# Feed-forward value chunks by seven block products instead of eight, in a fused two-model kernel on one core

## The chip, the core and the metric

One core of one Trainium2 chip runs the whole program: two small transformer blocks one after the other, batch 1, 512 tokens, model width 1024, all in float32. The metric is the device time of one execution in microseconds (us). The engines are TensorE (PE, matmuls; PEld is its weight load), VectorE (DVE), ScalarE (ACT), GpSimd (POOL) and SyncE (SP, here only a DMA queue). Each takes its own instructions in the order in which they were written.

## The reference, cut to what matters

The change lies in the feed-forward, which runs twice (layers 0 and 1 of the first block):

```python
def conv_ffn(x, w_up, conv_w, conv_b, w_down):      # x: 512 x 1024, w_up: 1024 x 5632, w_down: 2816 x 1024
    a, g = jnp.split(x @ w_up, 2, axis=-1)           # values a, gates g: 512 x 2816 each
    g = lax.conv_general_dilated(g, conv_w[:, None, :], (1,), ((2, 0),), ..., feature_group_count=D_FF) + conv_b
    return (jax.nn.gelu(g) * a) @ w_down
```

The result is added to alpha times x and goes through a layer norm. The order of the program is: even mixer, feed-forward 0, odd mixer, feed-forward 1, and then a gated linear recurrence and a retention layer.

## The kernel before, in words

Every product is made of three matmuls. A float32 operand is split into hi (a rounded copy, on ACT) and lo (the rest, a subtraction on DVE), and `mm3` (L273) adds hi times hi, hi times lo and lo times hi. X^T, the input with its 1024 features on partitions (8 k-tiles of 128) and its 512 tokens on columns, is kept as `xh` and `xl`.

**Weights.** `unit` lists a load of up to 1 MB into one of two raw buffers (`NRAW`), and `piece` one half of it (8 k-tiles x 128 columns, 1024 elements a partition) that is split into hi and lo. `pump` (L180) walks both lists as far as it can: a load is issued on SP as soon as the unit two places ahead of it has no piece left, and a piece is split (`split_piece`, L238 on ACT, L242 on DVE) while fewer than 5 split pieces are held. `get` (L254) gives up the pieces of the last chunk, pumps, and returns the next ones. As engines are in order, a split stands in ACT's and DVE's queues behind the work that was written before that `get`.

**Feed-forward** (`ffn`, L1127). The 22 chunks of 128 features are taken in pairs: two gate chunks, then the two value chunks of the same features. A chunk is 8 k-tiles x 3 matmuls of 512 columns into one of the 8 PSUM banks (`fm`, L281). `g_evac` (L1132) takes a gate chunk out of PSUM: ACT scales it (L1137), DVE adds the two shifted products of the convolution (L1138, L1139), ACT applies the gelu (L1140). `a_evac` (L1143) multiplies the value chunk by it on DVE (L1145) and splits the result into hi and lo (L371 ACT, L372 DVE). The first four chunks run in two halves of 256 tokens, as the transposed tokens of the layer norm before come in (`fms` with `split`, L291). After the first 12 chunks the down projection adds their part to the residual (`tm`, two halves of 512 columns); the last 10 go through `out_proj` (L1045), whose second half runs token tile by token tile (`tail=5`: 5 weight pieces of 2 chunks held), with the layer norm of each tile following on DVE, ACT and POOL (L403, L415 to L425, and for layer 1 also a root-mean-square norm, L443 to L451) and its transposes at `middle()` and after the last tile. After the first part the kernel also issues loads of the norm's parameters on ACT's queue (L430), in layer 1 the parameters of the recurrence (`lru_params`, L1787, a chain of small DVE operations with one exponential on ACT) and in layer 0 one table copy on POOL's queue (L531).

In the feed-forwards POOL has nothing to do except the layer norms at either end.

Of the kernel before, what the change touches and what calls it, by code (L numbers as in the profile page):

```python
# [28 lines left out]
SPL = 4  # L29
# [84 lines left out]
class Core:  # L114
# [4 lines left out]
    def __init__(self, ctx, tc, io):  # L119
# [16 lines left out]
        self.next_raw = self.next_piece = self.cur = 0  # L136
        self.live = deque()
        self.nm = 0
        self.pending = deque()
# [35 lines left out]

    def piece(self, u, view, a, b, direct=False):
        self.units[u]["left"] += 1
        self.plist.append((u, view, a, b, direct))

    def pump(self, split=True):  # L180
        while True:
# [13 lines left out]
            n = self.next_piece  # L195
            if split and n < len(self.plist) and self.room():
                u, view, a, b, direct = self.plist[n]
# [53 lines left out]
    tight = spare = extra = 0  # L251
    held = 0

    def get(self, n=1):  # L254

# [9 lines left out]
        self.held = n  # L265
        self.pump()
        assert len(self.live) >= n
# [4 lines left out]

    def mm3(self, out, lhs, rhs, start, stop):  # L273
        (lh, ll), (rh, rl) = lhs, rhs
        mm = self.T.matmul
        mm(out, lh, rh, start=start, stop=False)  # L276
        mm(out, lh, rl, start=False, stop=False)  # L277
        mm(out, ll, rh, start=False, stop=stop)  # L278

# [10 lines left out]

    def fms(self, evacs, split=0):  # L291


        n = 0
        if split:
            self.flush(1)
            self.extra, self.eager = 0, False
            ws = self.get(split)
            pss = [self.ps() for _ in ws]
            for t0 in (0, 256):  # L300
                for k, (w, p) in enumerate(zip(ws, pss)):
                    if t0 or k == split - 1:
                        self.flush(3 if t0 else 2)
                    yield from self.fm(p, w, t0=t0, t1=t0 + 256)
                    if t0:
                        evacs[k](p)
                        if k == EAGER:
                            self.eager = True
                            self.pump()
            n = split  # L310
        for f in evacs[n:]:
            w, = self.get()
            p = self.ps()
            yield from self.fm(p, w)
            f(p)

    def tm(self, lhs, kpers, n, done, tail=3, pack=False, kind="mm", before=None, extra=2, middle=None):
# [809 lines left out]
    def ffn(self, l, rms=False):  # L1127
        A, V, al, fr = self.A, self.V, self.al, self.fr
        self.pool_lo = False
# [4 lines left out]
        def g_evac(c, p):  # L1134
# [8 lines left out]
        def a_evac(c, p):  # L1143
            acc = H[c]
            V.tensor_tensor(acc, p, acc, op=MUL)  # L1145
            hi, lo = al(F32R), al(F32R)
            self.split(hi, lo, acc)
            fr(acc)
            H[c] = hi, lo

        for part in self.FF_PARTS:
            fs = []
            for j in range(c0, c0 + part, 2):
                fs += [lambda p, c=c: g_evac(c, p) for c in (j, j + 1)] + [lambda p, c=c: a_evac(c, p) for c in (j, j + 1)]
            run(self.fms(fs, split=SPL if c0 == 0 else 0))
            if c0 == 0:
                gb = self.norm_params(l, 1)
                if rms:
                    g = self.bcast(self.io["norm_pre_2"][0])
                    self.lru_params()  # L1160
                if l == 0 and self.pre_rms:
                    self.table(4)
            lhs = lambda k, i: [t[:, i * 128:i * 128 + 128] for t in H[c0 + k]]
            first = c0 == 0
            if first:
                for h in range(2):
                    run(self.tm(lhs, [2] * (part // 2), 512, lambda i, p, h=h: self.residual(i, h, p), tail=0))
# [968 lines left out]
```

## Time and profile before

| | |
|---|---|
| median of 3 runs | 2002.61 us (2000.42 to 2003.55) |
| the profiled execution, its own time | 1997.43 us |
| its span, first to last instruction | 1995.5 us |
| busy share: PE, DVE, ACT, POOL | 98%, 50%, 41%, 21% |
| mean granted clock of TensorE | 0.996 of full speed |
| feed-forward 0, feed-forward 1 | about 300 to 665 us, 964 to 1328 us of the span |

A row of a timeline gives an instruction's start, its duration, engine, line, operation and tiles, and in brackets how long its engine had stood idle before it and on what. A matmul's duration includes its way through the array, so the rate of matmuls is read from start to start. Rows of groups give count, busy time, the mean of one in ns, and idle time before them with what ended it.

### The profile page before, as it was taken

Reading aid. Unit: us, or ns where it says so; the run is one execution under the profiler, and the core shown is the slowest. Engines: PE = TensorE matmul, PEld = TensorE weight load, DVE = VectorE, ACT = ScalarE, POOL = GpSimd, SP = SyncE. Lnnn points to the kernel's source line nnn. Section 1 sums busy time; section 2 is a strip of 40 time slices with the busy share of each in tenths; the row PEclk is TensorE's granted clock in tenths of the full one; section 3 lists DMA queues with packets and bytes.
Section 4 is the critical chain, followed back from the end, with each engine's and each line's share of the span. In section 5 each row is a group of like instructions: output and inputs, shape, how many; then the busy total and the mean of one; then the engine's idle time right before and its main releaser. Section 6 shows DMA issues by size and latency. Waiting matters only on the chain.

```text
span 1995.5 us, 25737 instructions
## 1 busy us (share of the span) xinstructions
PE 1947.4 (98%) x10228; PEld 1623.8 (81%) x10228; DVE 991.2 (50%) x1692; ACT 817.5 (41%) x1451; POOL 417.6 (21%) x368
## 2 busy tenths in 40 slices
PE   8999989999999999999999999999998999999998
PEld 6678868888888988777888888888886888888887
DVE  3553255442444533763655344375667555455443
ACT  3455434331333344784333233256655533333331
POOL 0334441000000264474300000031443211011000
PEclk9999999999999999999999999999999999999999
DMA  6432223232323433111232423232231322222221
GB/s 199 112 115 68 93 84 101 95 127 85 105 85 123 137 99 122 54 49 64 65 116 94 137 85 105 85 106 70 71 89 70 133 85 90 90 85 90 85 75 52
DMA packets 174164, 189.22 MB, mean 95 GB/s; under 512 B 15080, under 2 KB 133662, under 8 KB 174045
## 3 DMA queue, kind: packets, MB, share of 16 engines
q1 hardware_dynamic: 158044, 165.63, 26.2%
q10 hardware_dynamic: 12064, 17.37, 2.9%
q0 software_dynamic: 3936, 4.59, 0.7%
q8 instruction: 80, 1.31, 0.3%
q14 instruction: 40, 0.32, 0.0%
HBM read 182.19 MB, written 6.65 MB: 95 GB/s over the span
## 4 chain that ended last, share of the span: by engine, by line
PE 80%; DVE 8%; ACT 3%; issue 2%; SPq 2%; DMA 2%; POOL 2%; ACTq 0%; DVEq 0%; POOLq 0%
PE p L276 24%; PE p L277 24%; PE p L278 24%; SPq L190 1%; PE p L1545 1%; PE p L1525 1%; PE p L1663 1%; SPq L851 1%; DVE s L1891 1%; POOL lo L240 1%; PE p L391 1%; PE p L786 1%; DVE s L1890 1%; PE p L366 1%; ACT hi L238 0%
## 5 line engine op out<-in xcount | busy, mean ns | idle before, releaser
L276 PE MATMUL p<-xh,hi 128*128 128x512 f32 (+1 forms) x1200 | 457.9, 382 | 0.7 <-ACT xh L371 0.7
L238 ACT CAST hi<-raw 128x1024 fp32r<-128x1024 f32 (+4 forms) x294 | 301.4, 1033 | 382.5 <-PE p L278 307.9
L277 PE MATMUL p<-xl,hi 128*128 128x512 f32 (+1 forms) x1200 | 454.3, 379 | 1.3 <-DVE xl L372 1.3
L278 PE MATMUL p<-xh,lo 128*128 128x512 f32 (+1 forms) x1200 | 454.3, 379 | 0.4 <-DVE lo L242 0.4
L242 DVE TENSOR_TENSOR lo<-raw,hi 128x1024 fp32r<-128x1024 f32 (+2 forms) x212 | 258.7, 1227 | 356.3 <-ACT hi L238 336.8
L276 PE MATMUL p<-hi,s 128*128 128x512 f32 (+1 forms) x728 | 285.7, 392 | 7.5 <-ACT s L371 4.8
L278 PE MATMUL p<-hi,s 128*128 128x512 f32 (+1 forms) x728 | 283.6, 390 | 0.0
L277 PE MATMUL p<-lo,s 128*128 128x512 f32 (+1 forms) x728 | 282.9, 389 | 0.0
L276 PEld LDWEIGHTS p<-xh,hi 128*128 128x128 f32 x1200 | 225.9, 188 | 44.7 <-ACT xh L371 1.4
L278 PEld LDWEIGHTS p<-xh,lo 128*128 128x128 f32 x1200 | 226.0, 188 | 43.1 <-DVE lo L242 0.6
L277 PEld LDWEIGHTS p<-xl,hi 128*128 128x128 f32 x1200 | 226.0, 188 | 42.8 <-DVE xl L372 2.1
L240 POOL TENSOR_TENSOR lo<-raw,hi 128x1024 fp32r<-128x1024 f32 (+3 forms) x82 | 191.2, 2339 | 329.2 <-ACT hi L238 259.6
L422 POOL TENSOR_TENSOR xtok<-xtok,b 128x512 f32<-128x512 f32 x16 | 26.1, 1629 | 712.9 <-ACT xtok L421 371.9
L276 PE MATMUL p<-hi,xh 128*128 128x512 f32 (+3 forms) x480 | 170.1, 354 | 1.5 <-ACT s L841 0.8
L277 PE MATMUL p<-lo,xh 128*128 128x512 f32 (+3 forms) x480 | 169.0, 352 | 0.5 <-DVE lo L242 0.5
L278 PE MATMUL p<-hi,xl 128*128 128x512 f32 (+3 forms) x480 | 168.8, 352 | 0.0
L276 PEld LDWEIGHTS p<-hi,s 128*128 128x128 f32 x728 | 137.1, 188 | 36.9 <-ACT s L371 6.2
L371 ACT CAST s<-s 128x512 fp32r<-128x512 f32 (+1 forms) x100 | 59.1, 597 | 260.8 <-DVE s L1145 122.7
L278 PEld LDWEIGHTS p<-hi,s 128*128 128x128 f32 x728 | 137.1, 188 | 30.0 <-DVE s L372 2.1
L277 PEld LDWEIGHTS p<-lo,s 128*128 128x128 f32 x728 | 137.1, 188 | 26.6
L276 PEld LDWEIGHTS p<-hi,xh 128*128 128x128 f32 x480 | 90.6, 189 | 14.3 <-issue 1.7
L277 PEld LDWEIGHTS p<-lo,xh 128*128 128x128 f32 x480 | 90.6, 189 | 11.7 <-DVE lo L242 0.8
(313 smaller groups left out, 2584.9 us busy)
## 6 DMA issues: line engine op xcount, KB each, us to landing
raw<-in_ffn_w_up_dram SPq DMA_DIRECT2D x44, 1024.0 KB, 5.1
raw<-in_ret_w_in_dram SPq DMA_DIRECT2D x24, 1024.0 KB, 5.1
raw<-in_ffn_w_down_dram SPq DMA_DIRECT2D x20, 1024.0 KB, 5.1
raw<-in_ev_w_in_dram SPq DMA_DIRECT2D x24, 512.0 KB, 5.3
raw<-in_lru_w_in_dram SPq DMA_DIRECT2D x24, 512.0 KB, 5.7
raw<-in_ret_w_out_dram SPq DMA_DIRECT2D x8, 1024.0 KB, 5.0
raw<-in_lru_w_out_dram SPq DMA_DIRECT2D x6, 1024.0 KB, 5.0
s<-in_od_cmp_w_dram ACTq DMA_DIRECT2D x16, 256.0 KB, 4.8
```

The costliest lines, as they stand in the source:

```text
L190: self.nc.sync.dma_start(dst(raw), src)
L238: self.A.copy(dh, x)
L240: self.G.tensor_tensor(dl, x, dh, op=SUB)
L242: self.V.tensor_tensor(dl, x, dh, op=SUB)
L276: mm(out, lh, rh, start=start, stop=False)
L277: mm(out, lh, rl, start=False, stop=False)
L278: mm(out, ll, rh, start=False, stop=stop)
L366: self.T.matmul(outs[e][:, :n], q[a][r, i * 128:i * 128 + 128], k[b][r, :n], start=j == 0, stop=j == 2)
L371: self.A.copy(hi, src)
L391: self.T.transpose(p[:, c * 128:(c + 1) * 128], halves[b][:, c * 128:(c + 1) * 128], self.ident)
L422: self.G.tensor_tensor(b, b, gb[0][:, 512:], op=MUL)
L786: T.matmul(o[:, i * 128:i * 128 + 128], st["pt"][:, k * 128:k * 128 + 128], va[k][:, h * 128:h * 128 + 128], start=k == 0, stop=k == i)
```

## The change

Value chunks of a pair j >= 4 are multiplied as a 2 x 2 block product in Winograd's form. With X^T cut in four quarters a(th, kh) (256 tokens x 512 features) and the 1 MB of value weights in four blocks b11, b12, b21, b22 (512 features x 128 columns), seven products of 12 matmuls of 256 columns take the place of eight.

- POOL forms the sums of X^T once per layer (`form_sums`): 4 additions of xh and xl before the first matmul, 12 operations when the last tokens are there, all on 128 x 512 elements. `part` splits a sum (2 ACT, 2 DVE operations on 512 elements); the four parts are put into `todo` and written one per chunk in the second pair.
- POOL forms the sums of the weights in the raw buffer (`post` in `seven`): after the first of now three pieces has been split, the corner b22 is split (512 elements), and four subtractions on 128 x 512 follow. The other two pieces are split from the changed buffer; `cool` and `most` put that off.
- `fm7` runs the products; three go into the same bank `x` on top of each other, with an ACT copy of it in between.
- The gelu of the second gate chunk of such a pair is written after the first product's copy.
- The down projection comes in three parts, after 6, 8 and 8 chunks, and `tail` is 4. The parameter loads, `lru_params` and the table copy are written after the first pair.

```diff
-    def piece(self, u, view, a, b, direct=False):
+    def piece(self, u, view, a, b, direct=False, post=None):
...
+    def seven(self, u):
+        v = lambda r: r.rearrange("p (k n) -> p k n", k=8)
+        def post(r):
+            w = v(r)
+            b11, b12, b21, b22 = w[:, :4, :128], w[:, :4, 128:], w[:, 4:, :128], w[:, 4:, 128:]
+            h, l = self.al(F32R), self.al(F32R)
+            self.split(h.rearrange("p (k n) -> p k n", k=4), l.rearrange("p (k n) -> p k n", k=4), b22)
+            self.corner.append((h, l))
+            self.G.tensor_tensor(b11, b12, b11, op=SUB)
+            self.G.tensor_tensor(b12, b22, b12, op=SUB)
+            self.G.tensor_tensor(b22, b22, b11, op=SUB)
+            self.G.tensor_tensor(b21, b21, b22, op=SUB)
+        for c, f in ((0, post), (0, None), (128, None)):
+            self.piece(u, lambda r, c=c: v(r)[:, :, c:c + 128], 8, 128, post=f)
...
+                        most -= 1
+                        if post is not None:
+                            post(raw)
+                            self.cool, most = 1, 0
...
-    def get(self, n=1):
+    def get(self, n=1, most=1000):
...
-        self.pump()
+        if self.cool and len(self.live) >= n:
+            self.cool, most = 0, 0
+        self.pump(most=max(most, n - len(self.live)))
...
+    def form_sums(self, early):
+        G, al, fr = self.G, self.al, self.fr
+        v = lambda t: t.rearrange("p (k n) -> p k n", k=2)
+        if early:
+            self.qs, self.sums = {}, {}
+        def whole(n, th, kh):
+            self.qs[n] = [al(), al()]
+            for c, t in enumerate(self.qs[n]):
+                x = [self.quarter(y, th, kh)[:, 2 * c:2 * c + 2] for y in (self.xh, self.xl)]
+                G.tensor_tensor(v(t), x[0], x[1], op=ADD)
...
+        def part(n):
+            hs, ls = [al(F32R), al(F32R)], [al(F32R), al(F32R)]
+            for h, l, t in zip(hs, ls, self.qs[n]):
+                self.split(h, l, t)
...
+        if early:
+            whole("a11", 0, 0)
+            whole("a12", 0, 1)
+            return
+        whole("a21", 1, 0)
+        whole("a22", 1, 1)
+        comb("s1", "a21", "a22", ADD, "a22")
+        comb("s3", "a11", "a21", SUB, "a21")
+        comb("s2", "s1", "a11", SUB, "a11")
...
+        self.todo.extend(lambda n=n: part(n) for n in ("s1", "s3", "s2", "s4"))
...
+    def fm7(self, evacs):
...
+        w, = self.get(most=0)
+        x, z, y, e = (self.ps() for _ in range(4))
+        t0, t1 = self.al(), self.al()
+        yield mm(x, blk(w, 0), a(0, 0))
+        A.copy(t0[:, :256], x[:, :256])
+        self.steps()
+        self.pump(most=1)
+        yield mm(z, blk(w, 1), a(0, 1))
+        V.tensor_tensor(t0[:, :256], t0[:, :256], z[:, :256], op=ADD)
+        w, v = self.get(2, most=1)
+        self.cool = 0
+        yield mm(x, blk(v, 1), s("s2"), False)
+        A.copy(t1[:, :256], x[:, :256])
+        yield mm(y, blk(w, 0), s("s1"))
+        yield mm(x, blk(v, 0), s("s3"), False)
+        A.copy(t0[:, 256:], x[:, :256])
+        V.tensor_tensor(t1[:, 256:], t0[:, 256:], y[:, :256], op=ADD)
+        yield mm(e, blk(w, 1), a(1, 1))
+        V.tensor_tensor(t0[:, 256:], t0[:, 256:], e[:, :256], op=ADD)
+        evacs[0](t0)
+        corner = self.corner.popleft()
+        yield mm(y, [lambda k, t=t: t[:, 128 * k:128 * k + 128] for t in corner], s("s4"), False)
+        self.fr(*corner)
+        V.tensor_tensor(t1[:, :256], t1[:, :256], y[:, :256], op=ADD)
+        evacs[1](t1)
...
-    FF_PARTS = (12, 10)
+    FF_PARTS = (6, 8, 8)
...
+                    if j > 2 and base == 0:
+                        self.seven(u)
+                        continue
...
-            A.activation(acc, acc, AF.Gelu_apprx_tanh)
+            gelu = lambda: A.activation(acc, acc, AF.Gelu_apprx_tanh)
+            if c % 2 and c > 3:
+                self.todo.append(gelu)
+            else:
+                gelu()
...
+                if j == 0:
+                    run(self.fms(gs + [lambda p, c=c: a_evac(c, p) for c in (j, j + 1)], split=SPL, sums=True))
+                    gb = self.norm_params(l, 1)
+                    if rms:
+                        g = self.bcast(self.io["norm_pre_2"][0])
+                        self.lru_params()
+                    if l == 0 and self.pre_rms:
+                        self.table(4)
+                    continue
+                if j == 2:
+                    for _ in self.fms(gs + [lambda p, c=c: a_evac(c, p) for c in (j, j + 1)]):
+                        self.steps(1)
+                    continue
+                run(self.fms(gs))
+                run(self.fm7([lambda p, c=c: a_evac(c, p, True) for c in (j, j + 1)]))
...
-                self.out_proj(lhs, [2] * (part // 2), gb, 1.0, (lambda i: self.rms_pre(i, g)) if rms else None, tail=5, extra=3)
+                self.out_proj(lhs, [2] * (part // 2), gb, 1.0, (lambda i: self.rms_pre(i, g)) if rms else None, tail=4, extra=3)
```

## Rows read from the trace of the kernel before

**Rows 1.** The page: busy time by engine, share of the span, instructions.

```profile
PE 1947.4 (98%) x10228; PEld 1623.8 (81%) x10228; DVE 991.2 (50%) x1692; ACT 817.5 (41%) x1451; POOL 417.6 (21%) x368
```

**Rows 2.** Busy time by stretch: PE, PEld, DVE, ACT, POOL, clock, DMA share, GB/s.

```profile
257.50:261.00 3.50, 3.50 (x24) 2.45 (x23) 0.69 (x1) 0.59 (x1) 2.88 (x7) 0.51 0.00 0
...
376.00:664.00 288.00, 288.00 (x1280) 238.74 (x1279) 132.56 (x160) 90.30 (x114) 8.84 (x6) 1.00 0.31 98
```

**Rows 3.** PE's timeline: matmuls of 256 and of 512 columns, first and last.

```profile
304.54 0.28 PE L276 MATMUL p<-xh,hi 128*128 128x256 f32 x1
...
305.98 0.28 PE L276 MATMUL p<-xh,s 128*128 128x256 f32 x1
...
345.62 0.39 PE L278 MATMUL p<-xh,lo 128*128 128x512 f32 x1
...
356.50 0.39 PE L278 MATMUL p<-xh,lo 128*128 128x512 f32 x1
```

**Rows 4.** Groups of instructions by shape, feed-forward 0, 376 to 664 us.

```profile
L242 DVE TENSOR_TENSOR lo<-raw,hi 128x1024 fp32r<-128x1024 f32 x49 | 60.0, 1225 | 88.6 <-ACT hi L238 88.6
L238 ACT CAST hi<-raw 128x1024 fp32r<-128x1024 f32 x49 | 51.3, 1046 | 71.9 <-PE p L278 67.2 <-DVE xtok L405 4.4 <-issue 0.3
...
L372 DVE TENSOR_TENSOR s<-s,s 128x512 fp32r<-128x512 f32 x16 | 11.1, 693 | 11.0 <-ACT s L371 11.0
...
L371 ACT CAST s<-s 128x512 fp32r<-128x512 f32 x16 | 10.0, 624 | 48.1 <-DVE s L1145 48.1
...
L423 POOL TENSOR_TENSOR xtok<-xtok,b 128x512 f32<-128x512 f32 x3 | 3.9, 1286 | 0.2
```

**Rows 5.** Groups of instructions by shape, 800 to 915 us: copies of 256 columns.

```profile
L1533 DVE COPY s<-p 128x256 f32<-128x256 f32 x12 | 5.1, 424 | 7.8 <-PE p L1525 6.9 <-POOL s L1518 0.8
L1533 ACT COPY s<-p 128x256 f32<-128x256 f32 x12 | 4.5, 372 | 5.3 <-PE p L1525 5.1
```

**Rows 6.** ACT's timeline in feed-forward 0: two splits, and a gate chunk's evacuation.

```profile
329.94 1.99 ACT L238 CAST hi<-raw 128x1024 fp32r<-128x1024 f32 x2
331.83 0.78 ACT L1137 ACTIVATE s<-p,par 128x512 f32<-128x512 f32 x1
...
353.53 0.78 ACT L1137 ACTIVATE s<-p,par 128x512 f32<-128x512 f32 x1 [3.14 <-PE p L278]
355.97 0.64 ACT L1140 ACTIVATE s<-s 128x512 f32<-128x512 f32 x1 [1.66 <-DVE s L1139]
356.51 1.03 ACT L238 CAST hi<-raw 128x1024 fp32r<-128x1024 f32 x1
```

**Rows 7.** DVE's and POOL's timelines, 303 to 309 us.

```profile
304.92 1.86 DVE L242 TENSOR_TENSOR lo<-raw,hi 128x1024 fp32r<-128x1024 f32 x1 [0.38 <-ACT hi L238]
...
304.02 1.67 POOL L422 TENSOR_TENSOR xtok<-xtok,b 128x512 f32<-128x512 f32 x1 [3.08 <-ACT xtok L421]
305.77 2.15 POOL L423 TENSOR_TENSOR xtok<-xtok,b 128x512 f32<-128x512 f32 x1
```

**Rows 8.** Timelines of ACT and DVE in feed-forward 1 where `lru_params` runs.

```profile
1101.15 1.28 ACT L1799 ACT_TABLE_LOAD   x1 [0.71 <-issue]
...
1101.08 0.17 DVE L1794 TENSOR_SCALAR hb<-par 128x24 f32<-128x24 f32 x1
...
1107.68 0.17 DVE L1813 TENSOR_SCALAR sp<-sp 128x12 f32<-128x12 f32 x1
```

**Rows 9.** PE's timeline: a wait of 3.7 us in the even mixer.

```profile
256.38 0.66 PE L994 MATMUL p<-s,s 128*64 128x128 f32 x8 [3.72 <-ACT s L985]
```

**Rows 10.** The page: loads of feed-forward weights, KB each, median us to landing.

```profile
raw<-in_ffn_w_up_dram SPq DMA_DIRECT2D x44, 1024.0 KB, 5.1
```

**Rows 11.** Timelines of DVE, POOL and PE at the end of feed-forward 1.

```profile
1311.75 0.68 DVE L403 TENSOR_TENSOR xtok<-xtok,p 128x512 f32<-128x512 f32 x1
...
1328.37 1.27 POOL L450 TENSOR_TENSOR s<-s,b 128x512 f32<-128x512 f32 x1
...
1329.69 0.66 PE L391 MATMUL p<-ident,s 128*128 128x128 f32 x4 [0.82 <-POOL s L450]
```

More of the change, by code (lines that the diff above doesn't have):

```diff
@@ L137, in __init__ @@
         self.live = deque()
+        self.corner = deque()
+        self.todo = deque()
         self.nm = 0
@@ L174, in unit, with pump @@
         return len(self.units) - 1
-    def piece(self, u, view, a, b, direct=False):
+    def piece(self, u, view, a, b, direct=False, post=None):
         self.units[u]["left"] += 1
-        self.plist.append((u, view, a, b, direct))
-    def pump(self, split=True):
+        self.plist.append((u, view, a, b, direct, post))
+    def seven(self, u):
[12 more added lines that the diff above has]
+            self.piece(u, lambda r, c=c: v(r)[:, :, c:c + 128], 8, 128, post=f)
+    def pump(self, split=True, most=1000):
         while True:
@@ L195, in pump @@
             n = self.next_piece
-            if split and n < len(self.plist) and self.room():
-                u, view, a, b, direct = self.plist[n]
+            if split and most and n < len(self.plist) and self.room():
+                u, view, a, b, direct, post = self.plist[n]
                 raw = self.units[u]["tile"]
@@ L289, in fm, with fms @@
                 yield self.step * 3 * 216 * (t1 - t0) // 512
-    def fms(self, evacs, split=0):
+    def fms(self, evacs, split=0, sums=False):
         n = 0
@@ L296, in fms @@
             self.flush(1)
+            if sums:
+                self.form_sums(True)
             self.extra, self.eager = 0, False
@@ L303, in fms @@
                         self.flush(3 if t0 else 2)
+                    if t0 and k == 0 and sums:
+                        self.form_sums(False)
                     yield from self.fm(p, w, t0=t0, t1=t0 + 256)
@@ L315, in fms, with quarter, comb @@
             f(p)
+    def quarter(self, x, th, kh):
+        return x[:, 4 * kh:4 * kh + 4, 256 * th:256 * th + 256]
+    def form_sums(self, early):
[8 more added lines that the diff above has]
+                G.tensor_tensor(v(t), x[0], x[1], op=ADD)
+        def comb(n, a, b, op, out):
+            for x, y, t in zip(self.qs[a], self.qs[b], self.qs[out]):
+                G.tensor_tensor(t, x, y, op=op)
+            self.qs[n] = self.qs.pop(out)
+        def part(n):
+            hs, ls = [al(F32R), al(F32R)], [al(F32R), al(F32R)]
+            for h, l, t in zip(hs, ls, self.qs[n]):
+                self.split(h, l, t)
+            self.sums[n] = hs, ls
+            fr(*self.qs.pop(n))
+        if early:
[7 more added lines that the diff above has]
+        comb("s2", "s1", "a11", SUB, "a11")
+        s4 = [al(), al()]
+        for x, y, t in zip(self.qs["a12"], self.qs["s2"], s4):
+            G.tensor_tensor(t, x, y, op=SUB)
+        fr(*self.qs.pop("a12"))
+        self.qs["s4"] = s4
+        self.todo.extend(lambda n=n: part(n) for n in ("s1", "s3", "s2", "s4"))
@@ new lines, in steps, with fr_sums, a, s @@
+    def steps(self, n=1000):
+        while n and self.todo:
+            self.todo.popleft()()
+            n -= 1
+    def fr_sums(self):
+        for hs, ls in self.sums.values():
+            self.fr(*hs, *ls)
+    def fm7(self, evacs):
+        V, A = self.V, self.A
+        def a(th, kh):
+            return lambda k: (self.quarter(self.xh, th, kh)[:, k], self.quarter(self.xl, th, kh)[:, k])
+        def s(n):
+            hs, ls = self.sums[n]
+            return lambda k: tuple(t[k // 2][:, 256 * (k % 2):256 * (k % 2) + 256] for t in (hs, ls))
+        def mm(p, b, x, start=True):
+            for k in range(4):
+                self.mm3(p[:, :256], (b[0](k), b[1](k)), x(k), start and k == 0, k == 3, on=not start)
+            return 12 * 120
+        def blk(w, r):
+            return [lambda k, t=t: t[:, 4 * r + k] for t in w]
+        w, = self.get(most=0)
[23 more added lines that the diff above has]
+        evacs[1](t1)
@@ L1151, in ffn @@
         for part in self.FF_PARTS:
-            fs = []
             for j in range(c0, c0 + part, 2):
[L1154 to L1162, printed above, removed]
+                gs = [lambda p, c=c: g_evac(c, p) for c in (j, j + 1)]
+                if j == 0:
[13 more added lines that the diff above has]
+                run(self.fm7([lambda p, c=c: a_evac(c, p, True) for c in (j, j + 1)]))
+            if c0 + part == 22:
+                self.fr_sums()
             lhs = lambda k, i: [t[:, i * 128:i * 128 + 128] for t in H[c0 + k]]
-            first = c0 == 0
-            if first:
+            alpha = ALPHA if c0 == 0 else 1.0
+            if c0 + part < 22:
                 for h in range(2):
-                    run(self.tm(lhs, [2] * (part // 2), 512, lambda i, p, h=h: self.residual(i, h, p), tail=0))
+                    run(self.tm(lhs, [2] * (part // 2), 512, lambda i, p, h=h: self.residual(i, h, p, alpha), tail=0))
             else:
-                self.out_proj(lhs, [2] * (part // 2), gb, 1.0, (lambda i: self.rms_pre(i, g)) if rms else None, tail=5, extra=3)
+                self.out_proj(lhs, [2] * (part // 2), gb, 1.0, (lambda i: self.rms_pre(i, g)) if rms else None, tail=4, extra=3)
             for c in range(c0, c0 + part):
```

15 lines of the change are left out of this document (9 added, 6 removed).

## The prediction, made before the changed kernel was run

> **What bounds the kernel now.** The page comes first: PE is busy 98% of the span, DVE 50%, ACT 41%, POOL 21% [rows 1]. The question is then whether the feed-forwards have any idle PE time that a change could fill. By stretches they have none: from 376 to 664 us PE is busy 288.00 of 288.00 us at full clock, while DVE works 133 us, ACT 90 and POOL 9 [rows 2]. So fewer matmuls shorten it one for one, and every wait that PE did not have before lengthens it one for one.
>
> **What is removed.** A matmul costs its start-to-start time. 48 of 512 columns take 10.88 us, 0.227 each; 12 of 256 columns take 1.44 us, 0.120 each, not half [rows 3]. Two value chunks are 48 matmuls of 512 columns, 10.88 us; seven products are 84 of 256 columns, 10.08 us. A pair saves 0.80 us, 9 pairs in each of 2 layers 14.4 us. The Trainium skill (TensorE: Matmul & The Clock Gate, section "Back-to-back issue gap") gives N ÷ 2.4 GHz plus 2.5 ns for a gap at full clock, that is 215.8 and 109.2 ns: by it a pair would save 1.19 us and the sum below would be 7 us lower. These rows have 11 ns more at both widths, so the measurement decides.
>
> **What is added in a steady pair** (20.98 us: two gate chunks at 5.45, seven products at 1.44). ACT gets a third split (1.05), a corner split (0.62) and three copies of 256 columns (0.37 each); DVE a third lo (1.23), a corner lo (0.69) and five sums of 256 columns (0.42 each); POOL four operations of 1.29 [rows 4, 5]. All that lies beside PE's work, but product 5 goes into the bank that ACT copies after product 3, and ACT is in order. With 0 at the second gate chunk's end: evacuation at 0.21, gelu 2.44 later at 2.65, the next start 0.54 later, splits 0.95 apart [rows 6]. So the next gate piece is split from 3.19, the next value piece from 4.14, its corner from 5.09 and the copy runs from 5.62 to 5.99. PE, some 0.05 later, starts product 5 at 6.04 and not at 4 × 1.44 = 5.76: **0.28 us**. This holds for six pairs of a layer, the fourth to sixth and the eighth to tenth, each followed by another pair of its part. In the seventh and eleventh one split of down-weights stands there in place of value piece and corner, and the copy is early; the third is counted below. 12 × 0.28 = 3.4 us.
>
> POOL's four subtractions must end before the second and third value pieces are split. They share something with DVE: where a DVE subtraction of two SBUF operands met POOL's additions, it took 1.86 us and not 1.23, ending 1.09 after POOL's first ended at 305.69, and POOL's second took 2.15, ending 1.14 after DVE [rows 4, 7]. So I let such operations exclude each other, the waiting one starting with about 0.15 us of head start. DVE reads from PSUM I leave free. Laid out so, the pieces are ready 6 us or more before product 3 of the next pair needs them, hidden by its gate chunks; if that cover is gone, a pair waits up to the four operations' 5.2 us.
>
> **What is added at the start of a layer.** I followed the queues in the order in which they are written, with these durations; without the change that order gives chunk 2's evacuation at 331.8 and chunk 4's at 353.5, as the rows have it [rows 6]. In feed-forward 0 POOL is free from about 308 [rows 7], so its 16 sums at 1.29 last to about 333. Each two-operand DVE operation of pairs 1 and 2 waits for one of them, and ACT behind it: chunk 2 is evacuated 4 us later. Then come four parts (8 × 0.53 on ACT, 8 × 0.61 on DVE, issue to issue), the last ones between the third pair's POOL operations. Evacuation of chunk 5 begins 4.4 us late at 363.3, the copy of product 1 stands behind it and ends at 364.4, and product 3, due at 361.7, **waits 2.8 us**. Product 5 then waits 1.7 for the second copy, behind a gelu and two splits of down-weights. Together 4.5 us. (Bounds: 0 if POOL and DVE do not hinder each other; 7.1 if the waiter has no head start.)
>
> In feed-forward 1 the same place also gets `lru_params`, which before ran beside the down projection: 6.7 us of small DVE operations one behind the other, and a table load of 1.28 on ACT, with another when the gelu comes back [rows 8]. Everything behind it moves 7.3 us: product 3 **waits 10.1 us**, product 5 again 1.7. (Bounds: 4.9 and 1.7 without the POOL conflict; 12.6 and 1.7.) After a wait of 3.7 us PE's granted clock was 0.51 of full, the lower of its two levels, for 3.5 us [rows 9, 2]; that costs 1.7 once more (0 to 3).
>
> **What moves.** The two parameter loads are 0.8 us of ACT issue, inside the lag above. POOL's table copy goes behind the sums, some 25 us later; its reader is the next mixer, 300 us away. On SP the load of the next value weights is issued after the third piece's lo instead of the second's, about 7 us into a pair; with 5.1 to landing [rows 10] it is there at 12 and wanted at 15. The third part adds 8 residual additions a layer, 0.69 each, on DVE beside the next matmuls: 0, or 11 for both layers if uncovered.
>
> `tail=4` shortens each token tile of the last pass from 6.8 to 5.45 us. In feed-forward 0 the norms still fit. In feed-forward 1 the chain is DVE's: from its first residual at 1311.75 to the end of token tile 1 on POOL at 1329.64 is 17.9 us, and PE waits 0.82 for it [rows 11]. The pass began at 1328.3 − 4 × 6.8 − 0.8 = 1300.2, so the chain started 11.5 us into it, behind the splits of the next stage's weights, whose load was issued only after the last down-weights' split. With four pieces held that split comes 5 us earlier and its load is no longer waited for; four splits on DVE then end 8.4 us into the pass (3.4 for residuals before them, 4 × 1.25). The chain ends at 8.4 + 17.9 = 26.3; before, 29.4, with 5.45 us more matmuls in it. 26.3 + 5.45 − 29.4 = **+2.3 us** (0 to 5).
>
> **Sum.** −14.4 + 3.4 + 4.5 + 11.8 + 1.7 + 2.3 = +9.3 us. The profiled execution's 1997.43 becomes 2006.7. It lies 5.2 below the median of the runs; on that median the forecast is 2002.6 + 9.3 = 2011.9 us.
>
> **Rivals.** A change under 0.2% (4 us) can't be told from none here.
> - *The start lag is hidden.* If the second pair's slack takes up the sums and `lru_params`, only the 0.28 waits and the tail stay: −14.4 + 3.4 + 2.3 = −8.7, 1993.9 us. For it: DVE is at 46% and ACT at 31% of the stretch [rows 2]. Against: evacuations go to and fro between the two, so their waits add. It decides from the point at which product 1's copy ends less than 1.4 us after product 1.
> - *POOL and DVE do not hinder each other* on these strided operands. Then only `lru_params` is left: 4.9 + 1.7 at product 3 and 5, −14.4 + 3.4 + 6.6 + 2.3 = −2.1, 2000.5 us: the same. Against it stands the pair in [rows 7].
> - *The waiter gets no head start.* The lag then lasts through the steady pairs (about 1.2 at product 5): my schedule's waits are 14 and 22 us in the two layers, −14.4 + 36 + 4 = +25.6, 2028 us. The 1.09 against 1.23 speaks against it.
>
> **How the numbers follow.** Forecast 0.47 (own range +4 to +20), hidden lag 0.25, no conflict 0.21, no head start 0.07. Faster is the hidden lag and a little of the third: 0.28; the same, most of the third and the forecast's low edge: 0.24; slower 0.48. The range is 1993, the fastest rival, to 2023, forecast's far bounds; left out are the last rival and the tails beyond the first.
>
> **What would show it.** Right: products at 0.120 start to start; a PE wait of 9 to 12 us on ACT's copy before the third product of the third pair of feed-forward 1, of 2 to 4 in feed-forward 0, and 0.3 before product 5 in pairs 4 and later; DVE two-operand rows of 1.8 us beside POOL. Wrong: no wait over 1 us at product 3, or waits at gate chunks, which I have at none.

## The result, and the profile after

Over four runs each, the changed kernel takes 2020.48 us in the median (2018.31 to 2021.76), the kernel before 2001.51: a ratio of 1.0089, 95% interval 1.0076 to 1.0102. It is slower, as forecast, but by 19 us and not by 9. The profiled execution took 2018.31 us, its span is 2016.5.

PE's times from start to start show where. Each stretch runs from the first matmul behind the third token tile's transposes at the start of a stage to the same place in the next; the start of the recurrence stage runs from its first matmul to the first of its second token half.

| stretch | before, from | before, us | after, us | difference |
|---|---|---|---|---|
| even mixer, start of feed-forward 0 | 0 | 309.66 | 312.91 | +3.25 |
| feed-forward 0 | 309.66 | 364.94 | 372.80 | +7.86 |
| odd mixer | 674.60 | 299.01 | 298.70 | -0.31 |
| feed-forward 1 | 973.61 | 357.38 | 365.87 | +8.49 |
| start of the recurrence | 1330.99 | 15.02 | 16.77 | +1.75 |
| the rest | 1346.01 | 642.62 | 642.64 | 0.0 |

The first row is nearly all code that did not change. In the runs below it came out between 311.5 and 314.6, and the profiled execution of before, at 1997.43 us, is 4 us under its median, so it was probably a quick one there. The change itself shows as +17.8 us in the four rows behind it.

The page of the changed kernel, busy time by engine, beside [rows 1]:

```profile
PE 1944.0 (96%) x10876; PEld 1650.2 (82%) x10876; DVE 1090.7 (54%) x1832; ACT 866.6 (43%) x1557; POOL 570.6 (28%) x472
```

PE is busy 3 us less in a span that is 21 us longer, so waits outweigh the saving (whether the saving itself was made is read from run 8 below). They lie in three places. The first is PE's timeline between product 2 and product 3 of the third pair, in feed-forward 0 and in feed-forward 1:

```profile
364.78 0.28 PE L307 MATMUL p<-xh,lo 128*128 128x256 f32 x1
375.60 0.58 PE L305 MATMUL p<-s,hi 128*128 128x256 f32 x1 [10.54 <-ACT s L435]
...
1036.29 0.28 PE L307 MATMUL p<-xh,lo 128*128 128x256 f32 x1
1046.11 0.58 PE L305 MATMUL p<-s,hi 128*128 128x256 f32 x1 [9.54 <-ACT s L435]
```

From start to start, less the 0.12 of a matmul, 10.70 and 9.70 us are lost, both on the copy after product 1 (L435), as forecast; but feed-forward 0 was to wait 2.8. What ACT did there (its timeline):

```profile
347.57 0.63 ACT L1283 ACTIVATE s<-s 128x512 f32<-128x512 f32 x1 [2.28 <-DVE s L1282]
356.04 1.05 ACT L263 CAST hi<-raw 128x1024 fp32r<-128x1024 f32 x1 [7.84 <-DMA raw<-in_ffn_w_up_dram]
356.99 0.61 ACT L511 CAST s<-raw 128x512 fp32r<-128x512 f32 x1
...
374.51 0.77 ACT L1280 ACTIVATE s<-p,par 128x512 f32<-128x512 f32 x1
375.19 0.36 ACT L435 COPY s<-p 128x256 f32<-128x256 f32 x1
```

ACT stands 7.84 us on the load of the third pair's value weights, and all behind it is late. SP issued that load at 338.15, so it took 17.9 us, against 5.1 in [rows 10]. What is beside it is in SP's and POOL's timelines (the first line is the load, the last one POOL's timeline before the change) and in the table of stretches (us of PE, PEld, DVE, ACT, POOL, then granted clock, DMA share, GB/s):

```profile
338.15 0.37 SPq L211 DMA_DIRECT2D raw<-in_ffn_w_up_dram  x1
...
332.39 3.01 POOL L397 TENSOR_TENSOR s<-s,s 128x512 f32<-128x512 f32 x2
335.33 1.11 POOL L671 DMA_DIRECT2D scr<-flat  x1
358.43 1.67 POOL L193 TENSOR_TENSOR raw<-raw 128x512 f32<-128x512 f32 x1 [21.99 <-DVE lo L267]
...
307.87 1.11 POOL L531 DMA_DIRECT2D scr<-flat  x1
```

```profile
334.00:340.00 6.00, 6.00 (x28) 4.99 (x27) 4.63 (x7) 4.34 (x6) 2.44 (x2) 1.00 0.58 168
340.00:346.00 6.00, 6.00 (x28) 4.95 (x28) 4.27 (x7) 3.29 (x5) 0.00 (x0) 1.00 0.74 242
346.00:352.00 6.00, 6.00 (x28) 4.99 (x27) 1.44 (x3) 0.63 (x1) 0.00 (x0) 1.00 0.69 233
...
370.00:376.00 6.00, 0.40 (x2) 0.40 (x3) 4.00 (x6) 2.96 (x5) 0.00 (x0) 0.51 0.29 89
...
1042.00:1048.00 6.00, 1.89 (x9) 1.89 (x10) 4.05 (x6) 2.60 (x5) 0.00 (x0) 0.50 0.27 90
...
1350.00:1356.00 6.00, 5.58 (x24) 5.28 (x25) 5.27 (x9) 3.99 (x10) 3.17 (x3) 0.50 0.01 3
```

POOL issues the table copy (1280 KB from DRAM to DRAM) when it is through with its sums, at 335.33; before, it went out at 307.87 and had landed at 324.1, just as the next load was issued (324.24). Now it and two parameter loads of 512 KB are under way together with the value load; runs 1 and 2 test which of them stretches it. Behind each long wait the clock stands at its lower level (0.51 and 0.50 in the stretches), and the products from there on took another 2.17 and 1.88 us.

The second place is the steady pair: PE's and ACT's timelines of the fifth pair, between product 4 and product 5.

```profile
455.45 0.28 PE L307 MATMUL p<-s,lo 128*128 128x256 f32 x1
455.82 0.39 PE L305 MATMUL p<-s,hi 128*128 128x256 f32 x1
```

```profile
452.46 0.63 ACT L1283 ACTIVATE s<-s 128x512 f32<-128x512 f32 x1 [0.63 <-DVE s L1282]
453.00 1.98 ACT L263 CAST hi<-raw 128x1024 fp32r<-128x1024 f32 x2
454.89 0.61 ACT L511 CAST s<-raw 128x512 fp32r<-128x512 f32 x1
455.40 0.36 ACT L443 COPY s<-p 128x256 f32<-128x256 f32 x1
```

From start to start, less the 0.12 of a matmul, this is 0.24 us, with the put-off gelu, two splits and the corner ahead of the copy. It stands in exactly the six pairs of each layer that were named, and besides in the third pair of feed-forward 1 (0.26). As the first matmul behind it is 0.1 slower, a pair loses up to 0.35.

The third place is the end of feed-forward 1 (PE's timeline; the last line is of the kernel before):

```profile
1343.30 0.66 PE L531 MATMUL p<-ident,s 128*128 128x128 f32 x4 [0.69 <-POOL s L590]
...
1349.04 0.66 PE L531 MATMUL p<-ident,s 128*128 128x128 f32 x4 [1.70 <-POOL s L590]
...
1350.28 0.58 PE L305 MATMUL p<-xh,hi 128*128 128x256 f32 x1 [0.59 <-ACT xh L511]
...
1330.99 0.39 PE L276 MATMUL p<-xh,s 128*128 128x256 f32 x1 [0.64 <-ACT xh L371]
```

The kernel before had two waits here, the 0.82 of [rows 11] and this 0.64; now there are three. The last one, 0.59, is not new: new are the first, 0.69, and the growth of the second from 0.82 to 1.70.

Two-operand DVE operations beside POOL's take longer again, as in [rows 7] (DVE's timeline: two lo's beside POOL's sums, two with POOL idle, two parts beside its weight subtractions, where one alone takes 0.69):

```profile
326.31 3.71 DVE L267 TENSOR_TENSOR lo<-raw,hi 128x1024 fp32r<-128x1024 f32 x2 [2.98 <-ACT hi L263]
...
336.89 2.36 DVE L267 TENSOR_TENSOR lo<-raw,hi 128x1024 fp32r<-128x1024 f32 x2 [0.55 <-ACT hi L263]
...
358.86 3.49 DVE L512 TENSOR_TENSOR s<-s,s 128x512 fp32r<-128x512 f32 x2
```

The Trainium skill (SBUF — State Buffer, section "SBUF: two separate sides") says that a GpSimd operation and a DVE operation with two SBUF inputs take a shared pair of ports in turn, each for its whole instruction; these rows agree (1.86 us for a lo beside POOL's sums, 1.18 beside an idle POOL).

### The profile page after: what moved, and what is told of

It reads as the page before. It is cut to its first block, busy times and chain, and to the rows that moved or that the text cites. A ratio compares the mean times of both kernels' runs of the same rounds, so it can differ in the third digit from the quotient of the medians.

```text
span 2016.5 us, 27443 instructions
## 1 busy us (share of the span) xinstructions
PE 1944.0 (96%) x10876; PEld 1650.2 (82%) x10876; DVE 1090.7 (54%) x1832; ACT 866.6 (43%) x1557; POOL 570.6 (28%) x472
## 4 chain that ended last, share of the span: by engine, by line
PE 66%; DVE 15%; ACT 7%; DMA 4%; POOL 3%; issue 3%; SPq 2%; ACTq 0%; DVEq 0%; POOLq 0%
PE p L305 19%; PE p L306 19%; PE p L307 19%; ACT hi L263 3%; DVE lo L267 2%; SPq L211 2%; DVE s L512 2%; PE p L1702 1%; PE p L1682 1%; DMA raw<-in_ffn_w_up_dram 1%; ACT s L511 1%; DVE s L1292 1%; PE p L1820 1%; DVE s L1282 1%; POOL s L376 1%
## 5 line engine op out<-in xcount | busy, mean ns | idle before, releaser
L263 ACT CAST hi<-raw 128x1024 fp32r<-128x1024 f32 (+4 forms) x312 | 316.1, 1031 | 382.6 <-PE p L307 260.8
L267 DVE TENSOR_TENSOR lo<-raw,hi 128x1024 fp32r<-128x1024 f32 (+1 forms) x230 | 281.4, 1237 | 323.0 <-ACT hi L263 322.4
L305 PE MATMUL p<-xh,hi 128*128 128x512 f32 (+1 forms) x1128 | 408.5, 362 | 1.8 <-ACT xh L511 1.8
L306 PE MATMUL p<-xl,hi 128*128 128x512 f32 (+1 forms) x1128 | 404.9, 359 | 2.1 <-DVE xl L512 2.0
L307 PE MATMUL p<-xh,lo 128*128 128x512 f32 (+1 forms) x1128 | 404.1, 358 | 0.0
L305 PEld LDWEIGHTS p<-xh,hi 128*128 128x128 f32 x1128 | 214.5, 190 | 35.9 <-ACT xh L511 3.2
L307 PEld LDWEIGHTS p<-xh,lo 128*128 128x128 f32 x1128 | 214.5, 190 | 31.2
L193 POOL TENSOR_TENSOR raw<-raw 128x512 f32<-128x512 f32 x18 | 29.3, 1626 | 440.6 <-DVE lo L267 440.6
L512 DVE TENSOR_TENSOR s<-s,s 128x512 fp32r<-128x512 f32 (+1 forms) x116 | 92.4, 808 | 56.9 <-ACT s L511 55.8
L305 PE MATMUL p<-s,hi 128*128 128x256 f32 (+1 forms) x272 | 86.3, 317 | 21.7 <-ACT s L435 20.1
```

What stands on the lines that cost most here:

```text
L193: self.G.tensor_tensor(b11, b12, b11, op=SUB)
L263: self.A.copy(dh, x)
L267: self.V.tensor_tensor(dl, x, dh, op=SUB)
L305: mm(out, lh, rh, start=start, stop=False, skip_group_check=on)
L306: mm(out, lh, rl, start=False, stop=False, skip_group_check=on)
L307: mm(out, ll, rh, start=False, stop=stop, skip_group_check=on)
```

## The experiments

Ratios are to the kernel before, run on the same chip at the same time.

**1. The table copy alone** (a1) is moved: into the gap between POOL's two groups of sums.

```diff
             whole("a12", 0, 1)
+            if self.pre_rms and 4 not in self.scr:
+                self.table(4)
             return
...
-                    if l == 0 and self.pre_rms:
-                        self.table(4)
```

> The changed kernel with one thing moved: POOL's copy of the bias table goes between the two groups of sums (POOL was idle there, 316 to 318 us) instead of behind all of them. Theory (the copy runs into the load of the third pair's value weights and stretches it from 5 us to 17): the load lands about 5 us after its issue, the wait before the third product of the third pair in feed-forward 0 falls from 10.70 us to 2 to 4, the 2.17 us at half clock behind it to under 1, product 5 there waits up to 1.7; the kernel gains 6.5 to 10 us on the changed one (about 2012). Feed-forward 1, which has no table copy, keeps its 9.70 and 1.88. Rival (the sums on POOL and the queue of ACT and DVE make the wait by themselves): the wait in feed-forward 0 stays over 9 us and the time within 2 us of the changed kernel's.

Measured: ratio 1.0033 (1.0021 to 1.0045), 2010.43 us. PE's, ACT's and POOL's timelines in feed-forward 0:

```profile
363.95 0.28 PE L307 MATMUL p<-xh,lo 128*128 128x256 f32 x1
366.81 0.39 PE L305 MATMUL p<-s,hi 128*128 128x256 f32 x1 [2.58 <-ACT s L437]
...
371.45 0.38 PE L305 MATMUL p<-s,hi 128*128 128x256 f32 x1 [1.51 <-ACT s L445]
```

```profile
346.72 0.63 ACT L1285 ACTIVATE s<-s 128x512 f32<-128x512 f32 x1 [2.28 <-DVE s L1284]
347.26 1.03 ACT L263 CAST hi<-raw 128x1024 fp32r<-128x1024 f32 x1
```

```profile
315.27 1.11 POOL L673 DMA_DIRECT2D scr<-flat  x1
```

The split no longer waits for the load. Product 3 waits 2.74 and product 5 1.67, start to start; the forecast had 2.8 and 1.7. The granted clock read 1.00 from 364 to 376 us. Feed-forward 0 fell from 372.80 to 364.53 us, feed-forward 1 stayed (365.86 against 365.87). So the table copy's place is what made feed-forward 0 lose more than forecast.

**2. The parameters alone** (a2): the parameter loads and `lru_params` go behind the seventh pair.

```diff
                 run(self.fm7(...))
+                if j == 12:
+                    gb = self.norm_params(l, 1)
+                    if rms:
+                        g = self.bcast(self.io["norm_pre_2"][0])
+                        self.lru_params()
```

> The changed kernel with the layer-norm parameter loads and lru_params moved from behind the first pair to behind the seventh, ahead of a down projection; the table copy stays. Theory (lru_params alone is what feed-forward 1 has over the plain lag): the wait before the third product of the third pair in feed-forward 1 falls from 9.70 us to 2 to 4, the 1.88 at half clock to under 1; product 5 waits up to 1.7; a gain of 5 to 9 us. In feed-forward 0 the table copy still runs into the load, so 8 to 11 us stay there. Rival (the parameter loads share the DMA engines and are part of the stretched load): feed-forward 0 falls by 2 us or more as well. Second rival (lru_params was hidden and the sums are the cause): feed-forward 1 keeps over 8 us.

Measured: 1.0027 (1.0017 to 1.0037), 2008.83 us. In feed-forward 1 the wait is 2.02 at product 3 and 1.67 at product 5, and the stretch fell from 365.87 to 358.41, 7.46 us. In feed-forward 0 the wait fell from 10.70 to 8.88 and the stretch from 372.80 to 370.68: the 2 us or more that the first rival named, so the parameter loads have a part in it. Some 0.7 of it is ACT's time for issuing them: that much the wait falls from run 1 to run 3, where no load is late. The other 1.1 is the load itself, as ACT's wait on it shows, 6.69 in place of 7.84:

```profile
354.63 1.05 ACT L263 CAST hi<-raw 128x1024 fp32r<-128x1024 f32 x1 [6.69 <-DMA raw<-in_ffn_w_up_dram]
```

Issued at 337.88, it still took 16.8 us beside the table copy alone.

**3. Both moves** (a3).

> Both moves together. Theory: each layer keeps only the lag of the sums that the prediction laid out, 2.8 us before the third product of the third pair and up to 1.7 before the fifth; with 14.4 saved, 3 to 4 lost in the twelve steady pairs and 2 to 5 at the end of feed-forward 1, the kernel comes to 2002 to 2007, equal to the kernel before or up to 0.3% slower. Rival (POOL and DVE do not hinder each other, the whole lag came from the table and lru_params): no wait over 0.5 us in either third pair, 1997 to 2000, faster than before by 0.1 to 0.2%.

Measured: 0.9995 (0.9986 to 1.0003), 2002.85 us: the same as before, in the theory's range. The waits at product 3 are 2.07 and 2.03; the rival without any is out. In feed-forward 1 product 5 did not wait this time, and yet the stretch is that of run 2 to a hundredth (358.41): the clock fell behind the 2.03, and PE came to product 5 late by itself. From product 3 to the down projection run 2 takes 9.06 us at full clock with the wait of 1.67, and this run 9.05 at the lower clock without it. Stretches of this run and, last, of run 2 behind the same wait:

```profile
1034.00:1038.00 4.00, 4.00 (x25) 3.80 (x25) 2.67 (x3) 2.51 (x4) 0.00 (x0) 0.72 0.07 8
```

```profile
1037.00:1042.00 5.00, 3.49 (x29) 3.29 (x28) 3.27 (x5) 2.78 (x4) 0.00 (x0) 1.00 0.01 3
```

**4. Both moves, and seven products from the fourth pair on** (a4).

```diff
-                    if j > 2 and base == 0:
+                    if j > 4 and base == 0:
...
-            if c % 2 and c > 3:
+            if c % 2 and c > 5:
...
-                if j == 2:
+                if j in (2, 4):
```

> Both moves, and the third pair goes back to plain products, so that seven products begin with the fourth pair. Theory (2.8 + 1.7 us of waits a layer against 0.8 saved by a pair): 7 us faster than the run with both moves (5 to 8), 1995 to 1999, about 0.2% faster than the kernel before; no PE wait over 0.5 us on ACT in the third and fourth pair. Rival (the lag of the sums lasts, the third pair only takes the wait first): the fourth pair's product 3 then waits 1.5 us or more, and the time is within 3 us of the run with both moves.

Measured: 0.9951 (0.9939 to 0.9964), 1993.87 us: faster than before. The third pair does not wait, and the fourth only the 0.24 of a steady one, so the lag of the sums is over by then. Feed-forward 0 takes 360.73, 4.21 less than before; eight pairs by 0.80 less six by 0.35 is 4.3. The gain on run 3 is 9 us, over the 5 to 8 expected: by the profiles 6.2 lie in the two feed-forwards, and 3.1 where no edit was made, in the odd mixer (1.8) and the start of the recurrence (1.3).

**5. POOL's last eight sums made, but read by nobody** (b4, on run 3); the four parts are split from the plain quarter sums, so the kernel leaves those eight sums out of what it computes.

```diff
-        comb("s1", "a21", "a22", ADD, "a22")
...
+        idle = [al(), al()]
+        for a, b, op in (("a21", "a22", ADD), ("a11", "a21", SUB), ("a22", "a11", SUB), ("a12", "a22", SUB)):
+            for x, y, t in zip(self.qs[a], self.qs[b], idle):
+                G.tensor_tensor(t, x, y, op=op)
+        fr(*idle)
+        for n, a in (("s1", "a21"), ("s3", "a22"), ("s2", "a11"), ("s4", "a12")):
+            self.qs[n] = self.qs.pop(a)
```

> On the version with both moves and seven products from the third pair on (label a3_both): POOL does its sixteen sums as before, but the last eight are written to two tiles that nobody reads, and the four parts are split from the plain quarter sums; so the computation lacks those eight sums, and no instruction waits for them. Theory (POOL's two-operand operations hold up DVE's, and ACT behind it, whether anybody reads them): the third pair's product 3 still waits 1.5 to 2.8 us on ACT's copy in both layers, as in a3_both (2.07 and 2.03). Rival (the lag is the parts waiting for late sums): that wait falls under 0.5 us, and the kernel is 6 us or more faster than a3_both.

Measured: 0.9993 (0.9984 to 1.0002). POOL's timeline, and PE's waits in feed-forward 0 and, last, 1 (total, times, longest):

```profile
322.95 12.50 POOL L397 TENSOR_TENSOR s<-s,s 128x512 f32<-128x512 f32 x8
```

```profile
PE p L305 <- ACT s L436: 2.0, 1, 2.0
PE p L305 <- ACT s L444: 1.5, 1, 1.5
...
PE p L305 <- ACT s L436: 1.9, 1, 1.9
```

Start to start 2.12 and 2.05, as in run 3. So the lag is not a wait for these late sums. That POOL stretches DVE's operations is in the DVE rows above; a layer with POOL wholly idle was not tried, so how much of the 2 us is stretching and how much the four parts' own work on ACT and DVE is not separated by a run.

**6. The gelu at once** (b1, on run 4; `self.todo.append(gelu)` becomes `gelu()`).

> On the version that begins with the fourth pair (label a4_from_fourth): the second gelu of a pair is no longer put off but issued behind its convolution, as in the kernel before. Theory (ACT is in order, and the gelu waits for DVE's two convolution steps with the copy of product 1 behind it): product 3 of all eight pairs of a layer waits 0.7 us, product 5 no longer waits; 16 x 0.74 against 12 x 0.24 to 0.29 is 8 to 9 us slower than a4_from_fourth (ratio to the kernel before 0.995 becomes 0.999). Rival (the copy's place in ACT's queue does not matter, as product 2 covers it): no wait at product 3, time as a4_from_fourth.

Measured: 1.0006 (0.9998 to 1.0015), 11 us slower than run 4. ACT's timeline, and PE's waits in feed-forward 0:

```profile
440.79 0.63 ACT L1285 ACTIVATE s<-s 128x512 f32<-128x512 f32 x1 [1.66 <-DVE s L1284]
441.33 0.35 ACT L437 COPY s<-p 128x256 f32<-128x256 f32 x1
```

```profile
PE p L305 <- ACT s L437: 4.4, 8, 0.6
```

Eight waits a layer, 0.71 each start to start (one of them 0.92); both feed-forwards grow by 4.4 us, and the start of the recurrence, at the lower clock this time, by 2.4, where no gelu stands. Putting the gelu off is worth 8.8 us, more than half of the 12.8 that the seven products of run 4 save.

**7 and 8. The order of the copy** (b2 and d2, on run 4). First only the corner and POOL's subtractions go behind the copy after product 3 (`post` is kept in a list until then):

> On a4_from_fourth: the corner split and POOL's four subtractions of the next pair are issued behind the copy after product 3 instead of ahead of it. Theory (product 5's 0.24 us is the corner's split on ACT standing ahead of the copy): the twelve waits of 0.24 fall to 0.16 or less, 2 to 4 us faster than a4_from_fourth; POOL's subtractions end about 0.5 us later, still covered. Rival (POOL's later subtractions hold DVE's lo's and the second and third value piece): waits of 0.3 us or more appear at product 3 or 7 or at a gate chunk, and nothing is gained.

Measured: 0.9948 (0.9935 to 0.9962), no faster than run 4 within the interval. The feed-forwards are 0.6 us shorter each; nine waits of 0.15 to 0.24 are left at product 5, some of them now in pairs that had none. ACT still has the gelu and two splits ahead of the copy, and in these pairs DVE makes a lo ahead of its convolution, so that the gelu waits 1.10 us for it and not 0.64. The gain expected was too large: the gelu's place, which comes from DVE's convolution, sets the copy's, not the corner alone. Then the whole next value piece goes behind:

```diff
-        w, v = self.get(2, most=1)
-        self.cool = 0
+        w, v = self.get(2, most=0)
         yield mm(x, blk(v, 1), s("s2"), False)
         A.copy(t1[:, :256], x[:, :256])
+        self.pump(most=1)
+        self.cool = 0
```

> The copy's place alone, on a4_from_fourth. Theory: both feed-forwards 1.75 us shorter, the wait of 0.90 at the end of feed-forward 1 comes back with 1.91 and 0.80 behind it; 2 to 4 us faster than a4_from_fourth, ratio 0.993 to 0.9945, about 1 us behind d1_copy_first_extra. Rival (the waits of 0.24 cost nothing, as a stall elsewhere takes them up): the time is that of a4_from_fourth.

Measured: 0.9950 (0.9934 to 0.9965), 1992.09 us. No wait at product 5 in any pair; feed-forward 0 takes 358.97 and feed-forward 1 353.40, 1.76 and 1.91 less than in run 4. The stretches show the gain; the median gained 1.8 us, which the intervals can't tell from none.

**9. The spare weight pieces later** (b3, on run 4: `extra` is 0 in the last pass and 3 from behind its third token tile).

> On a4_from_fourth: in the last pass of feed-forward 1 the three spare weight pieces of the next stage are split behind the third token tile's norm instead of ahead of the first. Theory (the end of feed-forward 1 is a chain on DVE that begins behind those splits, 3.7 us of DVE for six half pieces): the waits of 0.90 and 1.91 us on POOL and 0.80 on ACT fall to under 1.5 us together; 2 to 3 us faster than a4_from_fourth. Rival (the chain is only as late as its token tiles' matmuls, or the next stage wants the pieces): the waits stay, or return as waits on ACT's hi or DVE's lo in the first 24 matmuls of the next stage; time the same within 1 us.

Measured: 0.9989 (0.9980 to 0.9998), 7 us slower than run 4. PE's waits at the end of feed-forward 1:

```profile
PE p L536 <- DVE s L596: 6.3, 1, 6.3
PE p L305 <- ACT xh L516: 1.3, 1, 1.3
```

The wait of 0.69 is gone, but the six splits (3.70 us on DVE from 1321.28) now stand ahead of the second token tile's norm, and PE waits 6.3 for that. The expected gain became a loss.

**10 to 12. The spare slots earlier** (on run 4): `self.extra = 3` before the last down projection, in both layers with the copy's order of run 8 (c1), in both without it (c2), and in feed-forward 1 alone with it (d1).

> On a4_from_fourth, two edits. (1) In the seven products the copy after product 3 is issued ahead of the whole next value piece (split, corner and POOL's subtractions), not only ahead of the corner. Theory (b2_corner_late left that piece's split, 0.95 us on ACT, ahead of the copy): no wait over 0.1 us at product 5 in any of the sixteen pairs, the feed-forwards 1.5 us shorter each. (2) The three spare weight slots are opened at the start of the last down projection instead of at its last four pieces, so that of four splits that stood ahead of the last norms one is left. Theory (the DVE chain at the end of feed-forward 1 starts behind those splits): the waits of 0.90 + 1.91 + 0.80 us there fall to under 1.5 together. Both: 5 to 8 us faster than a4_from_fourth, 1986 to 1989, ratio 0.991 to 0.9925. Rival (the chain at the end is bound by its own four norms, the pieces only fill gaps; POOL's later subtractions hold up the value pieces): the end's waits stay, or new waits over 0.5 us stand at product 3 or at a gate chunk; ratio 0.994 or above.

> On a4_from_fourth, the second of these two edits alone. Theory: product 5 keeps its 0.24 us in six pairs of a layer; the waits of 0.90 + 1.91 + 0.80 us at the end of feed-forward 1 fall to under 1.5 together, 2 to 4.5 us faster than a4_from_fourth (ratio 0.993 to 0.994). Rival (the chain is bound by its own norms): the waits stay and the time is the same within 1 us.

> On a4_from_fourth: the copy after product 3 ahead of the next value piece in both layers, and the spare weight slots opened at the start of the last down projection in feed-forward 1 alone. In c1_best the same two edits made feed-forward 0 1.75 us and feed-forward 1 2.64 us shorter than in a4_from_fourth, and the mixer between them 6.9 us longer. Theory (that mixer's loss comes from the slots opened in feed-forward 0, whose pieces leave the next stage's first low parts behind GpSimd): the mixer is back at 298 to 300 us start to start, both feed-forwards keep their gain, no wait over 0.1 us at product 5: 3 to 6 us faster than a4_from_fourth, ratio 0.992 to 0.9935. Rival (the mixer's loss comes from the order of the copy): the mixer stays over 303 us and the ratio at 0.995 or above.

Measured: c1 0.9958 (0.9944 to 0.9972), c2 0.9991 (0.9980 to 1.0002), d1 0.9948 (0.9934 to 0.9961). The first expectation fell: of the waits at the end only the first went, 0.69 in the views (the expectations count the three from start to start, as 0.90, 1.91 and 0.80); 1.70 and 0.61 stayed, and a new one of 0.23 on DVE's residual came (d1). So the end is in the main bound by its own norms, as the rival had it. The second fell further: c2 is some 7 us slower than run 4, not faster. The odd mixer grew by 6.9 us in c1 and 4.8 in c2; PE's waits at its start in c1, and POOL's timeline there:

```profile
PE p L306 <- POOL lo L265: 2.1, 1, 2.1
PE p L305 <- ACT hi L263: 0.6, 1, 0.6
```

```profile
692.90 7.61 POOL L265 TENSOR_TENSOR lo<-raw,hi 128x816 fp32r<-128x816 f32 x3 [23.69 <-ACT hi L263]
```

Three lo's stand on POOL there, 2.5 us each, and PE waits for the first; in run 4 DVE makes these three in 2.85 us at 687.07. From 691 to 701 us, with these waits, the mean clock was 0.83. With the slots opened in feed-forward 1 alone the mixer is back at 298.70, as the third expectation's theory had it; its ratio was to be 0.992 to 0.9935 and came out a little above. d1 and run 4 are both about half a per cent faster than the kernel before and can't be told apart.

## Why the prediction was right in sign and too low

- **Saving of 0.80 a pair.** Right within a tenth: run 8, without waits at product 5, shows 5.97 us for eight pairs, 0.75 each.
- **Waits at product 5 in twelve steady pairs.** The mechanism and the pairs were right; 0.28 forecast, 0.24 measured, 0.35 with the slow restart. Run 8 removed them by the order that was said to make them.
- **Start of feed-forward 0, 2.8 + 1.7.** Right as far as it went: 2.74 and 1.67 once the table copy was out of the way. In the changed kernel 10.70 at product 3 and 2.17 behind it stood there instead, 12.9 for 4.5.
- **The step that failed** is in "What moves": "POOL's table copy goes behind the sums, some 25 us later; its reader is the next mixer, 300 us away", costed at nothing. Its reader was looked at, but not what else is on the DMA engines while it runs. The load of 5.1 us on which the next sentence rested was one without that company; it took 17.9. Run 1 shows 8.3 us for it in feed-forward 0. In the sentence ahead of it, the parameter loads, costed as ACT's issue time alone, cost about 1 us more beside that load.
- **Start of feed-forward 1, 10.1 + 1.7.** 9.70 at product 3, and 1.88 behind it, of which 0.26 is a wait at product 5: not 1.7, since PE came to it late, at the lower clock. Without `lru_params` and the parameter loads the wait at product 3 was 7.68 shorter (run 2), where 7.3 was worked out.
- **Clock, 1.7 once.** A term too many in feed-forward 1: the prediction added it to product 5's 1.7, but at the lower clock PE works through the time in which it would wait at product 5. Behind product 3 the third pair lost 1.87 or 1.88 in both layers of runs 1 to 3, at either clock, as in the changed kernel's feed-forward 1; only its feed-forward 0, with 2.17, lost 0.3 more. The prediction had nothing for the start of the recurrence, which took 1.75 more, with the clock at 0.50.
- **tail=4, +2.3.** The size holds: in run 4 feed-forward 1 gains 2.07 where feed-forward 0 gains 4.21, so 2.1. The mechanism only in part: with fewer splits ahead of the norms the new wait of 0.69 goes (d1), the growth of the second from 0.82 to 1.70 stays. That this is the norms' chain with fewer matmuls to hide behind is argued, not shown by a run with `tail=5`.
- **The rivals.** A hidden lag is excluded by run 3, and "POOL and DVE do not hinder each other" by the DVE rows; against no head start stand the steady pairs, which wait 0.24 and not the 1.2 of that rival, and the 2.74 of the third pair.

In sum: saving -14.4, steady pairs 4.2, third pairs 12.9 and 11.6, end 2.1 and start of the recurrence 1.75 make +18.1; the four stretches show +17.8. The result lies within the stated range, 1993 to 2023, but not because the range foresaw this: its upper end was made of the far bounds of other terms, and the table copy had none.

## What to carry to other kernels

When a step is moved in an in-order queue, look at what its DMAs meet at their new time, not only at who reads them: a transfer whose reader is far away can still stretch a load that is needed soon (5.1 us to 17.9 here). A saving of 0.7% in matmuls (14.4 us) is worth what the queues beside it leave of it; begin it only where the lag of its preparation is over (here one pair later: 1.6 us less saving for both layers, 7.8 less waiting, by runs 3 and 4). And write what PE waits for ahead of what merely has room in the same queue.

## What the runs showed of the hardware

- A copy of 1280 KB from DRAM to DRAM, issued by POOL, takes 16 us by itself (20.3 in the changed kernel) and stretched a load of 1024 KB from 5.1 to 16.8 us (run 2), with two parameter loads beside it to 17.9. The 16 DMA engines as a whole were not short: alone, the copy takes 0.21 of their time (before, 307 to 325 us), and the share was 0.58 to 0.74 with all of it under way. But from 350 to 354 us the copy's queue (q0) and SP's (q1) move the same number of packets, the copy's five times as large (packets, MB, share):

```profile
q0 software_dynamic: 68, 0.35, 20.8%
q1 hardware_dynamic: 68, 0.07, 4.9%
```

The Trainium skill (DMA: Bandwidth & Descriptors, section "Queues, rings and completion order") says that each DMA engine takes packets of its queues in turn; the equal counts agree with that, and so does the load's end, 0.4 us behind the copy's and not ahead of it. That the copy sits on a few of the engines, and the rest of the load waits for its turn there, would fit the share, but is not shown: no view here names the engines.

- Behind a wait of about 2 us the clock fell in one execution (0.72, run 3) and not in another (1.00, run 2) with the same work there. So too at the start of the recurrence, behind waits of 1.70 and 0.59 in both: 0.50 in the changed kernel (1350 to 1356 us, above), 1.00 in run 4. Its stretch:

```profile
1329.00:1335.00 6.00, 5.37 (x42) 5.17 (x43) 5.26 (x9) 3.97 (x10) 3.15 (x3) 1.00 0.00 0
```

The start of the recurrence took 14.4 us in four profiles (run 4, c1, d1, d2) and 15.6 to 16.9 in the other changed ones: up to 2.5 us between profiles with the same work there, as much as some of the gains looked for here.
